# Three of the four activation sums of Strassen's forms on GpSimd, with two signs turned

## The chip, the cores and the metric

The kernel runs as one launch on one core of a Trainium2 chip. The time is the device time of a launch in microseconds (us), the median of 3 runs. The engines are written as in the profile: PE is TensorE (matmuls), DVE VectorE, ACT ScalarE, POOL GpSimd, SP SyncE, which here only issues transfers.

## The reference

One decoder block in float32, depth 1, batch 1: 512 tokens of width 1024, 256 memory tokens, a feed-forward width of 2816.

```python
def swiglu(u, w_gate_up, w_down):
    gate, up = jnp.split(u @ w_gate_up, 2, axis=-1)
    return (jax.nn.silu(gate) * up) @ w_down

    h = h + hybrid_mixer(rmsnorm(h, mix_norm[l]), ...)          # SSD heads + causal pooling
    h = h + memory_cross_attention(rmsnorm(h, xattn_norm[l]), rmsnorm(mem, mem_norm[l]), ...)
    h = h + swiglu(rmsnorm(h, ffn_norm[l]), w_gate_up[l], w_down[l])
    return rmsnorm(h, final_norm)
```

The change is in the feed-forward part alone, the last two fifths or so of the launch (from about 455 us on).

## The kernel before

**Precision.** Each float32 product is made of three passes in the PE's fp32r type: high part by high part, low by high, high by low. For a weight quad of 128x1024, ACT casts the high part (`whi`, L203) and DVE subtracts it from the quad for the low part (`wlo`, L205). Activations are split in the same way.

**Strassen.** The feed-forward products use Strassen's seven block products. For each pair of 128-channel blocks an activation set consists of FA and FB, 128x512 each: FA holds x11 (columns 0 to 255, `lo_`) and x12 (`hi_`), the first 256 tokens of the two blocks; FB holds x21 and x22, the other 256 tokens. `forms` (L1174) makes the seven left-hand forms of a set from them, each as a high and a low part:

- forms 1 and 2 are x11 and x12 as they are: high part `H1` (ACT, tile t_xh), low part `L1` (DVE L1193, t_xl);
- M, tile t_x57, holds form 5 = x11 - x21 (L1189) and form 7 = x22 - x21 (L1190), with `H2` and `L2` as its parts;
- N, tile t_x64, holds form 6 = -M_lo - x22 (L1197) and form 4 = -N_lo - x12 (L1199), with `H3` and `L3`;
- form 3 is x22: `H4`, tile t_xq, with its low part in the second half (L1184).

`forms` is called for 15 sets: i = 0 to 3 from the output projection of the attention (`i_o`, L1054 fills FA and FB), i = 4 to 14 from the gated values (`i_turnff`: PE transposes into a PSUM tile ffT, ACT copies FB and FA out of it, L1167).

**Stages.** The feed-forward work goes through gate/up blocks g (U:0 to U:5; matmul outputs gA, gB, gC) and down blocks d (d:0 to d:2; outputs dA, dB, dC) in the order g:0, g:1, d:0, g:2, g:3, d:1, g:4, g:5, d:2. A down block needs the sets of the two gate/up blocks ahead of it; the last of these sets are made while the down block already runs: i = 6 and 7 in d:0, 10 and 11 in d:1, 13 and 14 in d:2. The products within a block run in the order 1, 2, 5, 6, 3, 7, 4. After each product the PSUM result is added to its target: by DVE into the residual tiles t_hT in a down block (L1259), by ACT and DVE into t_gu tiles in a gate/up block, where ACT applies SiLU (L1118).

**Weights.** Four quads of each block matrix lie in memory; the seven weight forms are sums of them. For f = 5 and f = 7 a base quad is loaded on SP (L161, `raw<-w_s`) and a second one is added to it by a transfer that accumulates, issued on POOL (L172, `raw<-w_s`), which waits for the base to land. For f = 6 such a transfer on POOL adds one tile to another (L211, `wq<-raw`), for f = 3 and some f = 6 DVE does it (L194). There are six `raw` buffers, so a base load also waits until the tile that was in its buffer before has been read. Weights are cast and split one slot of the plan ahead of the products that use them.

**Order.** A list of slots (`SPEC`) sets which products, sets and weights belong together. Within that, the framework's scheduler fixes one list of instructions per engine ahead of the launch; an engine works through its list strictly from the top, and an instruction that waits holds up all behind it. Before the change POOL runs 66 instructions: a few fills at the start and 56 transfers that accumulate (38 at L172, 18 at L211).

Of the kernel before, what the change touches and what calls it, by code (L numbers as in the profile page):

```python
# [7 lines left out]
F32 = mybir.dt.float32  # L8
F32R = mybir.dt.float32r
AF = mybir.ActivationFunctionType  # L10
ALU = mybir.AluOpType
# [24 lines left out]

START = "x0 q0 h0 x1 h1 H0 q1 x2 x6 x3 q2 h2 q3 x4 q4 H1 q6 H2 q5 q7 a1 r0 x7 x5"
START_MM = "00 10 11 01 12 02 03 20 21 13 22 23 04 14 24 05 r 15 25 06 16 26 07 17 27"
# [23 lines left out]
def hybrid_block(ctx: ExitStack, tc: tile.TileContext, a: dict, out: bass.AP,  # L62
                 act_bufs=69, la=1, wb=(6, 4, 5), eng="", dact=(0, 1), raw_n=6, warm=12, spec=None, start=START, smm=START_MM, hu=1, dbg=None):
    nc = tc.nc
# [11 lines left out]
    def nm(base):  # L76
        uid[0] += 1
        return f"{base}_{uid[0]}"

    def T(base, dt=F32, n=512):  # L80
        return act.tile([P, n], dt, tag="a", name=nm("t_" + base))
# [141 lines left out]
    def need(*key):  # L223
        while key not in st:
            yield
# [35 lines left out]
    st = {}  # L261
# [778 lines left out]
    def i_o(m):  # L1040
        it = Item(keys=[("o", m)])

        def mm():
            proj(hold(it, "wo"), ready[("o", m)], [st["o", k] for k in range(8)])

        def post():
            h = st["h1", m]
            nc.vector.tensor_tensor(out=h, in0=h, in1=it.ps, op=ALU.add)
            yield
            i, c = m // 2, m % 2  # L1050
            if c == 0:
                st["F", i] = T("fa"), T("fb")
            for k in range(2):
                nc.scalar.activation(st["F", i][k][:, 256 * c:256 * c + 256], h[:, 256 * k:256 * k + 256],  # L1054
                                     AF.Identity, scale=col(V_FFN + m))
            yield
            if c == 1:
                yield from forms("fg", i, *st["F", i])

        it.mm, it.post = mm, post  # L1060
        return it
# [47 lines left out]
    def i_gu(b, f, part=None):  # L1109
        it, ends, width = product("g", b, f, part)  # L1110

        def add(base, tt, k):
            g = st[base, tt][:, :width]
            st["drained"] = nc.vector.tensor_tensor(out=g, in0=g, in1=it.ps[tt], op=ALU.add)  # L1114
            return g

        def gate(g, c):
            st["silu"] = nc.scalar.activation(g, g, AF.Silu, scale=st["r3",][:, c:c + 1])  # L1118

        def post():  # L1120
            if f in (1, 6, 5):
                for tt in range(2):
                    t = st["up"[f == 5] + str(f), tt] = T("gu")
                    nc.scalar.copy(t[:, :width], it.ps[tt])
            elif f in (2, 3):
                base, k = ("u1", 0) if f == 2 else ("u6", 1)
                gs = [add(base, tt, k) for tt in range(2)]
                yield
                yield from need("r3")
                for tt in range(2):  # L1130
                    gate(gs[tt], 2 * k + tt)
                    st["gate", k, tt] = st[base, tt]
            elif f == 7:
                us = [add("p5", tt, 1) for tt in range(2)]
                yield
                for tt in range(2):
                    nc.vector.scalar_tensor_tensor(out=us[tt], in0=us[tt], scalar=st["nr3",][:, 2 + tt:3 + tt],
                                                   in1=st["gate", 1, tt][:, :width], op0=ALU.mult, op1=ALU.mult)
                    st["fft", b, 1, tt] = st["p5", tt]
            else:  # L1140
                for tt in range(2):
                    g = st["gate", 0, tt][:, :width]
                    st["drained"] = nc.vector.scalar_tensor_tensor(
                        out=g, in0=it.ps[tt], scalar=st["nr3",][:, tt:tt + 1], in1=g, op0=ALU.mult, op1=ALU.mult)
                    st["fft", b, 0, tt] = st["gate", 0, tt]
            yield

        it.post = post if ends else None
        return it

    def i_turnff(b, i):

        it = Item()

        def mm():
            it.ps = psum.tile([P, 1024], F32, tag="pd", name=nm("ffT"), bufs=1)
            for k in (1, 0):
                for c in range(2):
                    for tt in range(2):
                        o = 512 * k + 256 * c + P * tt  # L1160
                        nc.tensor.transpose(it.ps[:, o:o + P], st["fft", b, k, tt][:, (2 * i + c) * P:(2 * i + c + 1) * P],
                                            ident)

        def post():
            F = T("fa"), T("fb")
            for k in (1, 0):
                nc.scalar.copy(F[k], it.ps[:, 512 * k:512 * k + 512])  # L1167
            yield
            yield from forms("ff", 2 * b + i, *F)

        it.mm, it.post = mm, post
        return it

    def forms(x, i, FA, FB):  # L1174

        lo_, hi_ = slice(0, 256), slice(256, 512)

        def cast(base, src, w=None):
            h = T(base, F32R)
            nc.scalar.copy(h if w is None else h[:, w], src)  # L1180
            return h

        def rest(dst, src, h):
            nc.vector.tensor_tensor(out=dst, in0=src, in1=h.bitcast(F32), op=ALU.subtract)  # L1184

        H1 = cast("xh", FA)
        H4 = cast("xq", FB[:, hi_], lo_)
        M = T("x57")
        nc.vector.tensor_tensor(out=M[:, lo_], in0=FA[:, lo_], in1=FB[:, lo_], op=ALU.subtract)  # L1189
        nc.vector.tensor_tensor(out=M[:, hi_], in0=FB[:, hi_], in1=FB[:, lo_], op=ALU.subtract)  # L1190
        yield
        L1 = T("xl", F32R)
        st["first rest"] = nc.vector.tensor_tensor(out=L1, in0=FA, in1=H1.bitcast(F32), op=ALU.subtract)  # L1193
        st["X", x, 1, i], st["X", x, 2, i] = (H1[:, lo_], L1[:, lo_]), (H1[:, hi_], L1[:, hi_])
        H2 = cast("xh", M)
        N = T("x64")
        nc.vector.scalar_tensor_tensor(out=N[:, lo_], in0=M[:, lo_], scalar=-1.0, in1=FB[:, hi_],  # L1197
                                       op0=ALU.mult, op1=ALU.subtract)
        nc.vector.scalar_tensor_tensor(out=N[:, hi_], in0=N[:, lo_], scalar=-1.0, in1=FA[:, hi_],  # L1199
                                       op0=ALU.mult, op1=ALU.subtract)  # L1200
        yield
        H3 = cast("xh", N)
        L2 = T("xl", F32R)
        rest(L2, M, H2)
        st["X", x, 5, i], st["X", x, 7, i] = (H2[:, lo_], L2[:, lo_]), (H2[:, hi_], L2[:, hi_])
        yield
        rest(H4[:, hi_], FB[:, hi_], H4[:, lo_])
        st["X", x, 3, i] = H4[:, lo_], H4[:, hi_]
        L3 = T("xl", F32R)
        rest(L3, N, H3)  # L1210
        st["X", x, 6, i], st["X", x, 4, i] = (H3[:, lo_], L3[:, lo_]), (H3[:, hi_], L3[:, hi_])
# [31 lines left out]
        return it  # L1243


    INTO = {1: (0, 0, 1), 2: (0, 0, 1), 6: (0, 1, 1), 5: (1, 1, -1), 7: (1, 1, -1), 3: (0, 1, 1), 4: (1, 0, -1)}

    def i_down(p, f, part=None):
        it, ends, _ = product("d", p, f, part)

        def post():
            r, k, sign = INTO[f]
            last = p == 2
            if last and f == 2:
                st["pre"] = nc.scalar.preload_act_table_set("natural_log_exp_and_others")
                after(st["pre"], st["silu"])
            for tt in range(2):
                h = st["h", 2 * k + tt, r]
                st["drained"] = nc.vector.tensor_tensor(out=h, in0=h, in1=it.ps[tt],  # L1259
                                                        op=ALU.add if sign > 0 else ALU.subtract)  # L1260
                if last and f in (2, 3, 7, 4):
                    squares(2 * k + tt, r)
                if last and f == 2:
                    gain(tt)
                if last and f == 4:
                    final([tt])
            if last and f == 7:
                gain(2)
                gain(3)
                final([2, 3])  # L1270
            yield
# [239 lines left out]
```

## Time and profile before

| what | value |
|---|---|
| time, median of 3 runs | 794.72 us (794.49 to 794.93) |
| profiled execution, span | 793.5 us |
| PE busy | 782.1 us, 99% of the span, 3780 matmuls |
| DVE busy | 635.8 us, 80%, 945 instructions |
| ACT busy | 498.4 us, 63%, 799 instructions |
| POOL busy | 49.9 us, 6%, 66 instructions |
| transfers | 128.60 MB, 162 GB/s over the span |

The profiled execution's own time is its span, 793.5 us; the median of the unprofiled runs is 1.2 us above it. A group's row reads: line, engine, operation, output tile <- input tiles, shape, count | busy time in us, mean ns of one | idle time of the engine ahead of them and what ended it. A timeline row reads: start, duration, engine, line, operation; in brackets the idle time of the engine just before it and what ended that. Names there lack their numbers, so M and N both read t_x. A row of windows gives, for each engine, the busy us and the number of instructions in that stretch, then PE's granted clock (1.00 is full speed), the share of time that the DMA engines were busy, and GB/s.

### The profile page before, as it was taken

The page shows a single profiled execution, that of the slowest core. Times are in us where ns is not written, and L with a number is a line of the kernel's source. Part 1 is how long each engine was busy: PE and PEld are TensorE (multiplying, and loading weights), DVE is VectorE, ACT ScalarE, POOL GpSimd, SP SyncE. Part 2 cuts the span into 40 slices and gives each one's busy share as a digit, 9 for nine tenths or more (in the row PEclk, how much of TensorE's full clock was granted, in tenths as well). Part 3 has the DMA queues.
Part 4 walks back from the last instruction along what each step waited for, and adds up shares of the span by engine and source line. Part 5 has one row for each costly group of instructions (what it writes and reads, how often), then busy time and mean ns, then how long its engine had stood idle before and what let it go on. Part 6 is the DMA issues. An engine that isn't in the chain of part 4 may idle for free.

```text
span 793.5 us, 10440 instructions
## 1 busy us (share of the span) xinstructions
PE 782.1 (99%) x3780; PEld 655.1 (83%) x3780; DVE 635.8 (80%) x945; ACT 498.4 (63%) x799; POOL 49.9 (6%) x66
## 2 busy tenths in 40 slices
PE   9999999999999999999999999999999999999995
PEld 7888888888888888888888888888888888888984
DVE  7999879999885799875766667788867698868897
ACT  8667699557953547555655695665445575455845
POOL 0000000000000000000000001011101011101000
PEclk9999999999999999999999999999999999999998
DMA  9235225133475234775446268688879697869602
GB/s 331 91 112 184 109 82 179 54 111 122 162 257 171 84 107 150 170 198 163 134 116 153 60 154 222 171 243 166 239 157 291 163 251 172 245 154 272 165 14 106
DMA packets 41282, 128.60 MB, mean 162 GB/s; under 512 B 4864, under 2 KB 7296, under 8 KB 41232
## 3 DMA queue, kind: packets, MB, share of 16 engines
q1 hardware_dynamic: 33024, 99.30, 37.0%
q0 software_dynamic: 8064, 28.58, 20.1%
q8 instruction: 29, 0.48, 0.2%
q14 instruction: 21, 0.17, 0.1%
q10 hardware_dynamic: 144, 0.07, 0.1%
HBM read 116.63 MB, written 2.13 MB: 150 GB/s over the span
## 4 chain that ended last, share of the span: by engine, by line
PE 92%; DVE 5%; issue 1%; DMA 1%; ACT 0%; SPq 0%; DVEq 0%
PE gA L1102 15%; PE gB L1102 8%; PE dA L1102 5%; PE gC L1102 4%; PE dB L1102 2%; PE xbc L117 2%; PE xbc L119 2%; PE xbc L118 2%; PE vAB L1102 2%; PE k L889 2%; PE z L117 2%; PE z L119 2%; PE op L117 2%; PE z L118 2%; PE wo L119 2%; PE op L118 2%
## 5 line engine op out<-in xcount | busy, mean ns | idle before, releaser
L203 ACT CAST whi<-raw 128x1024 fp32r<-128x1024 f32 (+1 forms) x125 | 129.0, 1040 | 91.1 <-PE wo L118 11.8
L205 DVE TENSOR_TENSOR wlo<-raw,whi 128x1024 fp32r<-128x1024 f32 (+1 forms) x125 | 149.8, 1208 | 28.2 <-ACT whi L203 27.3
L203 ACT CAST whi<-wq 128x1024 fp32r<-128x1024 f32 (+1 forms) x76 | 77.4, 1028 | 74.6 <-PE dA L1102 17.8
L205 DVE TENSOR_TENSOR wlo<-wq,whi 128x1024 fp32r<-128x1024 f32 (+1 forms) x76 | 90.3, 1194 | 38.7 <-ACT whi L203 38.6
L172 POOL DMA_DIRECT2D raw<-w_s x38 | 32.8, 867 | 646.0 <-DMA raw<-w_s 486.4
L1102 PE MATMUL gA<-whi,t_xh 128*128 128x512 f32 (+1 forms) x192 | 71.8, 374 | 0.0
L1102 PE MATMUL gA<-wlo,t_xh 128*128 128x512 f32 (+1 forms) x192 | 71.4, 372 | 0.0
L1102 PE MATMUL gA<-whi,t_xl 128*128 128x512 f32 (+1 forms) x192 | 71.3, 371 | 0.0
L1102 PEld LDWEIGHTS gA<-whi,t_xh 128*128 128x128 f32 x192 | 36.2, 188 | 6.6 <-ACT whi L203 0.4
L1102 PEld LDWEIGHTS gA<-wlo,t_xh 128*128 128x128 f32 x192 | 36.2, 188 | 6.3
L1102 PEld LDWEIGHTS gA<-whi,t_xl 128*128 128x128 f32 x192 | 36.2, 188 | 6.1
L1118 ACT ACTIVATE t_gu<-t_gu,s 128x512 f32<-128x512 f32 (+1 forms) x24 | 16.4, 688 | 35.9 <-DVE t_gu L1114 35.8
L194 DVE TENSOR_TENSOR wq<-wq,wq 128x1024 f32<-128x1024 f32 (+1 forms) x19 | 22.5, 1194 | 17.7 <-DMA wq<-raw 17.7
L1102 PE MATMUL dA<-whi,t_xh 128*128 128x512 f32 x88 | 34.1, 392 | 0.3 <-DVE t_hT L1259 0.2
L1102 PE MATMUL dA<-whi,t_xl 128*128 128x512 f32 x88 | 34.3, 389 | 0.0
L1102 PE MATMUL dA<-wlo,t_xh 128*128 128x512 f32 x88 | 34.1, 389 | 0.0
L1102 PE MATMUL gB<-whi,t_xq 128*128 128x512 f32 (+1 forms) x96 | 27.5, 371 | 0.0
L1180 ACT CAST t_xh<-t_x 128x512 fp32r<-128x512 f32 x30 | 18.6, 621 | 10.6 <-DVE t_x L1199 6.4
L117 PE MATMUL wo<-t_oh,whi 128*128 128x512 f32 x64 | 25.2, 394 | 0.0
L117 PE MATMUL v<-t_uh,whi 128*128 128x512 f32 x64 | 25.1, 392 | 0.0
L117 PE MATMUL z<-t_uh,whi 128*128 128x512 f32 x64 | 25.1, 392 | 0.0
L117 PE MATMUL q<-t_hgh,whi 128*128 128x512 f32 x64 | 25.1, 392 | 0.0
(401 smaller groups left out, 2221.2 us busy)
## 6 DMA issues: line engine op xcount, KB each, us to landing
raw<-w_u SPq DMA_DIRECT2D x68, 512.0 KB, 3.4
raw<-w_s SPq DMA_DIRECT2D x54, 512.0 KB, 4.6
wq<-w_s SPq DMA_DIRECT2D x36, 512.0 KB, 5.9
raw<-w_s POOLq DMA_DIRECT2D x36, 512.0 KB, 7.5
wq<-raw POOLq DMA_DIRECT2D x17, 512.0 KB, 8.6
t_x<-xT SPq DMA_DIRECT2D x16, 256.0 KB, 5.4
t_abc<-d_acs SPq DMA_DIRECT2D x16, 256.0 KB, 4.6
out<-t_hT SPq DMA_DIRECT2D x8, 256.0 KB, 2.3
```

The source lines that it names most:

```text
L117: nc.tensor.matmul(ps, whi, xhi, start=start, stop=False)
L118: nc.tensor.matmul(ps, whi, xlo, start=False, stop=False)
L119: nc.tensor.matmul(ps, wlo, xhi, start=False, stop=stop)
L172: nc.gpsimd.dma_start(sw[c, f][:, :n], quad("11" if f == 7 else "22"), accum_op=ALU.add)
L194: add = nc.vector.tensor_tensor(out=sw[c, 3][:, :n], in0=sw[c, 3][:, :n], in1=sw[c, 6][:, :n], op=ALU.add)
L203: nc.scalar.copy(hi[:, :n], raw[:, :n])
L205: nc.vector.tensor_tensor(out=lo[:, :n], in0=raw[:, :n], in1=hi.bitcast(F32)[:, :n], op=ALU.subtract)
L889: nc.tensor.matmul(it.ps[d], wh[:, ws], both, start=k == 0, stop=False, skip_group_check=True)
L1102: nc.tensor.matmul(it.ps[tt], p[:, ts_], w[:, ws], start=first, stop=(c, i, n) == pairs[-1] and p is xh and w is wl, skip_group_check=True)
L1118: st["silu"] = nc.scalar.activation(g, g, AF.Silu, scale=st["r3",][:, c:c + 1])
L1180: nc.scalar.copy(h if w is None else h[:, w], src)
```

## The change

`forms` has GpSimd make M_lo, M_hi and N_lo (L1187 to L1189 of the changed kernel); DVE keeps N_hi (now L1198), the low parts L1 (now L1195), L2, L3, and that of form 3 (now L1206). A plain subtraction gives N_lo only if M_lo is turned round, so form 5 is now x21 - x11, and form 3 is -x22 (ACT scales by -1 while it casts, L1192). The signs are taken back where the products are added up: `add` subtracts for f = 3 and f = 7 (its two other callers), the gate of f = 7 is multiplied by `r3` in place of its negative, and `INTO` turns the signs of 5 and 3. The tiles of M and N are also allocated ahead of those of H1 and H4. Nothing else is computed in another way. DVE's list goes from 937 rows to 892, POOL's from 71 to 116, ACT's and SP's keep their number (these lists count rows that a profile does not).

```diff
--- before.py
+++ after.py
@@ -1111,7 +1111,7 @@
 
         def add(base, tt, k):
             g = st[base, tt][:, :width]
-            st["drained"] = nc.vector.tensor_tensor(out=g, in0=g, in1=it.ps[tt], op=ALU.add)
+            st["drained"] = nc.vector.tensor_tensor(out=g, in0=g, in1=it.ps[tt], op=ALU.add if f == 2 else ALU.subtract)
             return g
 
         def gate(g, c):
@@ -1134,7 +1134,7 @@
                 us = [add("p5", tt, 1) for tt in range(2)]
                 yield
                 for tt in range(2):
-                    nc.vector.scalar_tensor_tensor(out=us[tt], in0=us[tt], scalar=st["nr3",][:, 2 + tt:3 + tt],
+                    nc.vector.scalar_tensor_tensor(out=us[tt], in0=us[tt], scalar=st["r3",][:, 2 + tt:3 + tt],
                                                    in1=st["gate", 1, tt][:, :width], op0=ALU.mult, op1=ALU.mult)
                     st["fft", b, 1, tt] = st["p5", tt]
             else:
@@ -1175,27 +1175,26 @@
 
         lo_, hi_ = slice(0, 256), slice(256, 512)
 
-        def cast(base, src, w=None):
+        def cast(base, src):
             h = T(base, F32R)
-            nc.scalar.copy(h if w is None else h[:, w], src)
+            nc.scalar.copy(h, src)
             return h
 
         def rest(dst, src, h):
             nc.vector.tensor_tensor(out=dst, in0=src, in1=h.bitcast(F32), op=ALU.subtract)
 
+        M, N = T("x57"), T("x64")
+        nc.gpsimd.tensor_tensor(out=M[:, lo_], in0=FB[:, lo_], in1=FA[:, lo_], op=ALU.subtract)
+        nc.gpsimd.tensor_tensor(out=M[:, hi_], in0=FB[:, hi_], in1=FB[:, lo_], op=ALU.subtract)
+        nc.gpsimd.tensor_tensor(out=N[:, lo_], in0=M[:, lo_], in1=FB[:, hi_], op=ALU.subtract)
         H1 = cast("xh", FA)
-        H4 = cast("xq", FB[:, hi_], lo_)
-        M = T("x57")
-        nc.vector.tensor_tensor(out=M[:, lo_], in0=FA[:, lo_], in1=FB[:, lo_], op=ALU.subtract)
-        nc.vector.tensor_tensor(out=M[:, hi_], in0=FB[:, hi_], in1=FB[:, lo_], op=ALU.subtract)
+        H4 = T("xq", F32R)
+        nc.scalar.activation(H4[:, lo_], FB[:, hi_], AF.Copy, scale=-1.0)
         yield
         L1 = T("xl", F32R)
         st["first rest"] = nc.vector.tensor_tensor(out=L1, in0=FA, in1=H1.bitcast(F32), op=ALU.subtract)
         st["X", x, 1, i], st["X", x, 2, i] = (H1[:, lo_], L1[:, lo_]), (H1[:, hi_], L1[:, hi_])
         H2 = cast("xh", M)
-        N = T("x64")
-        nc.vector.scalar_tensor_tensor(out=N[:, lo_], in0=M[:, lo_], scalar=-1.0, in1=FB[:, hi_],
-                                       op0=ALU.mult, op1=ALU.subtract)
         nc.vector.scalar_tensor_tensor(out=N[:, hi_], in0=N[:, lo_], scalar=-1.0, in1=FA[:, hi_],
                                        op0=ALU.mult, op1=ALU.subtract)
         yield
@@ -1204,7 +1203,8 @@
         rest(L2, M, H2)
         st["X", x, 5, i], st["X", x, 7, i] = (H2[:, lo_], L2[:, lo_]), (H2[:, hi_], L2[:, hi_])
         yield
-        rest(H4[:, hi_], FB[:, hi_], H4[:, lo_])
+        nc.vector.scalar_tensor_tensor(out=H4[:, hi_], in0=FB[:, hi_], scalar=-1.0, in1=H4.bitcast(F32)[:, lo_],
+                                       op0=ALU.mult, op1=ALU.subtract)
         st["X", x, 3, i] = H4[:, lo_], H4[:, hi_]
         L3 = T("xl", F32R)
         rest(L3, N, H3)
@@ -1243,7 +1243,7 @@
         return it
 
 
-    INTO = {1: (0, 0, 1), 2: (0, 0, 1), 6: (0, 1, 1), 5: (1, 1, -1), 7: (1, 1, -1), 3: (0, 1, 1), 4: (1, 0, -1)}
+    INTO = {1: (0, 0, 1), 2: (0, 0, 1), 6: (0, 1, 1), 5: (1, 1, 1), 7: (1, 1, -1), 3: (0, 1, -1), 4: (1, 0, -1)}
 
     def i_down(p, f, part=None):
         it, ends, _ = product("d", p, f, part)
```

The scheduler answers with another order. The place at which the prediction looks most is the set i = 6 at the start of d:0 (t_fa_1111_5197 and t_fb_1112_5198 are its FA and FB; set i = 7 is t_fa_1127_5249 and t_fb_1128_5250). First DVE, before:

```order
L205 TENSOR_TENSOR wlo_1139_5275<-wq_1098_5096,whi_1138_5274 128x1024
L1189 TENSOR_TENSOR t_x57_1117_5208<-t_fa_1111_5197,t_fb_1112_5198 128x256
L1190 TENSOR_TENSOR t_x57_1117_5208<-t_fb_1112_5198 128x256
L1193 TENSOR_TENSOR t_xl_1118_5212<-t_fa_1111_5197,t_xh_1115_5204 128x512
L1197 SCALAR_TENSOR_TENSOR t_x64_1120_5216<-t_x57_1117_5208,t_fb_1112_5198 128x256
L1184 TENSOR_TENSOR t_xq_1116_5206<-t_fb_1112_5198,t_xq_1116_5206 128x256
L1199 SCALAR_TENSOR_TENSOR t_x64_1120_5216<-t_x64_1120_5216,t_fa_1111_5197 128x256
L205 TENSOR_TENSOR wlo_1147_5316<-raw_1101_5104,whi_1146_5315 128x1024
L1184 TENSOR_TENSOR t_xl_1122_5221<-t_x57_1117_5208,t_xh_1119_5214 128x512
```

and now, with the start of set i = 7 at its end:

```order
L205 TENSOR_TENSOR wlo_1139_5275<-wq_1098_5096,whi_1138_5274 128x1024
L1198 SCALAR_TENSOR_TENSOR t_x64_1116_5205<-t_x64_1116_5205,t_fa_1111_5197 128x256
L205 TENSOR_TENSOR wlo_1147_5316<-raw_1101_5104,whi_1146_5315 128x1024
L1195 TENSOR_TENSOR t_xl_1119_5214<-t_fa_1111_5197,t_xh_1117_5209 128x512
L1206 SCALAR_TENSOR_TENSOR t_xq_1118_5211<-t_fb_1112_5198,t_xq_1118_5211 128x256
L1184 TENSOR_TENSOR t_xl_1122_5221<-t_x57_1115_5204,t_xh_1120_5216 128x512
L1184 TENSOR_TENSOR t_xl_1123_5224<-t_x64_1116_5205,t_xh_1121_5219 128x512
L205 TENSOR_TENSOR wlo_1150_5338<-wq_1075_4994,whi_1149_5337 128x1024
L1198 SCALAR_TENSOR_TENSOR t_x64_1132_5257<-t_x64_1132_5257,t_fa_1127_5249 128x256
L1195 TENSOR_TENSOR t_xl_1135_5266<-t_fa_1127_5249,t_xh_1133_5261 128x512
```

The one sum that DVE keeps (N_hi, L1198) now stands at the head of its set, ahead of a weight's low part (wlo_1147) and of L1 (t_xl_1119); before, L1 stood third in its set, and N_hi last.

POOL at the same place, before:

```order
L211 DMA wq_1075_4994<-raw_1092_5057 128x1024
L211 DMA wq_1095_5064<-raw_1101_5104 128x1024
L172 DMA raw_1166_5439<-w_s 128x1024
L172 DMA raw_1169_5446<-w_s 128x1024
L172 DMA raw_1184_5553<-w_s 128x1024
L172 DMA raw_1187_5560<-w_s 128x1024
```

and now:

```order
L211 DMA wq_1075_4994<-raw_1092_5057 128x1024
L211 DMA wq_1095_5064<-raw_1101_5104 128x1024
L172 DMA raw_1166_5439<-w_s 128x1024
L1187 TENSOR_TENSOR t_x57_1115_5204<-t_fb_1112_5198,t_fa_1111_5197 128x256
L1188 TENSOR_TENSOR t_x57_1115_5204<-t_fb_1112_5198 128x256
L1189 TENSOR_TENSOR t_x64_1116_5205<-t_x57_1115_5204,t_fb_1112_5198 128x256
L1188 TENSOR_TENSOR t_x57_1131_5256<-t_fb_1128_5250 128x256
L172 DMA raw_1169_5446<-w_s 128x1024
L1187 TENSOR_TENSOR t_x57_1131_5256<-t_fb_1128_5250,t_fa_1127_5249 128x256
L1189 TENSOR_TENSOR t_x64_1132_5257<-t_x57_1131_5256,t_fb_1128_5250 128x256
L172 DMA raw_1184_5553<-w_s 128x1024
```

The transfers keep their order. The three sums of set i = 6 stand behind the accumulation into raw_1166, and two of the sums of set i = 7 behind the one into raw_1169. At d:1 the lists have the same shape, with the sets i = 10 and 11.

ACT's list changes at this place too: the casts of M and N (H2, H3) of a set now follow each other, ahead of the cast of whi_1149 and of the copies of the next set's FB and FA. On PE the six dB matmuls of set i = 6 (form 5) now stand ahead of the dA and dC matmuls of set i = 7.

## The prediction

> **What bounds the kernel now.** I read the page first: busy times and the chain of work that ended last.
>
> ```profile
> PE 782.1 (99%) x3780; PEld 655.1 (83%) x3780; DVE 635.8 (80%) x945; ACT 498.4 (63%) x799; POOL 49.9 (6%) x66
> PE 92%; DVE 5%; issue 1%; DMA 1%; ACT 0%; SPq 0%; DVEq 0%
> ```
>
> PE is busy for 782.1 of 793.5 us, and the chain runs through it for 92%. Next, all that PE waits for in the whole span (columns: us in total, times, longest):
>
> ```profile
> PE warm L384 <- DVE ones L100: 1.2, 1, 1.2
> PE s L117 <- ACT whi L130: 0.8, 1, 0.8
> PE yo L119 <- DVE t_prl L241: 0.4, 1, 0.4
> PE dA L1102 <- DVE t_hT L1259: 0.2, 1, 0.2
> ```
>
> Where the change acts (L1102) PE waits for 0.2 us in all. So time taken off DVE buys at most 0.2 us there, plus what the tail behind the last matmul gives; anything that reaches PE too late costs its full lateness. Third, stretches: the end of gate/up blocks g:2 and g:3, the starts of d:0 and d:1, and the middle of d:2.
>
> ```profile
> 506.00:545.00 39.00, 39.00 (x190) 32.60 (x189) 33.24 (x48) 28.71 (x42) 5.13 (x6) 1.00 0.89 230
> 545.00:565.00 20.00, 19.86 (x88) 16.11 (x87) 18.61 (x27) 9.46 (x12) 1.72 (x2) 1.00 0.73 169
> 664.00:684.00 20.00, 19.86 (x88) 16.14 (x87) 18.87 (x26) 9.66 (x12) 1.72 (x2) 1.00 0.71 179
> 764.00:770.00 6.00, 6.00 (x28) 4.97 (x27) 6.00 (x11) 3.87 (x7) 0.00 (x0) 1.00 0.00 0
> ```
>
> DVE (fourth figure) has 5.8 us free in the first, but only 1.4 and 1.1 us in the two starts and none in d:2. There a delay on DVE can't be made up.
>
> **What is removed and added.** Groups of DVE and POOL:
>
> ```profile
> L1193 DVE TENSOR_TENSOR t_xl<-t_fa,t_xh 128x512 fp32r<-128x512 f32 x15 | 10.3, 686 | 0.1
> L1189 DVE TENSOR_TENSOR t_x<-t_fa,t_fb 128x256 f32<-128x256 f32 x15 | 6.3, 420 | 1.2 <-ACT t_fa L1167 0.9
> L172 POOL DMA_DIRECT2D raw<-w_s x38 | 32.8, 867 | 646.0 <-DMA raw<-w_s 486.4 <-DVE t_p L997 54.0 <-DVE t_hT L1259 38.7
> L109 POOL TENSOR_SCALAR_AFFINE_SELECT cmask<-cmask 128x128 f32<-128x128 f32 x1 | 0.3, 289 | 0.0
> L1503 POOL MEMSET const-float32-0.0<- 128x1 f32 x1 | 0.1, 100 | 0.3 <-issue 0.3
> ```
>
> DVE loses 45 sums of 420 ns (L1189 stands for the three lines): 18.9 us busy. They start 0.34 us apart (timelines below), so the real relief is 45 x 0.34 = 15.3 us, 1.0 us per set. By the second paragraph it is worth nothing, since PE's work covers it; only in d:2, where DVE never rests, could 1.0 us show.
>
> The trace has no GpSimd sum of two inputs. Lower bound: DVE's own 0.42 us. Upper: the select reads one input; less the 0.10 us of an almost empty POOL instruction it takes 0.19 us for 128 columns, or 0.48 us for 256 with the 0.10; a sum that reads its two inputs one after the other would take 0.10 + 2 x 0.38 = 0.86 us. I take 0.66, between the two; per set 3 x 0.66 + 0.1 for the links = 2.1 us. The Trainium skill (GPSIMD Engine Reference, Engine selection) advises against this very move: elementwise work of two inputs belongs on VectorE, GpSimd being about twice as slow. By its 2.6 cycles per element a sum would be about 0.65 us (an estimate from that page), and the total the same.
>
> **What is moved: sums behind transfers.** This decides. POOL works strictly in order, and the three sums of set 6 stand behind the accumulation into raw_1166; DVE's kept sum L1198 needs the last of them, and behind it on DVE wait the weight part wlo_1147 and L1. POOL around d:0, and SP's issues of the two base loads:
>
> ```profile
> 538.39 0.86 POOL L211 DMA_DIRECT2D wq<-raw  x1 [6.49 <-DVE wlo L205]
> 545.51 0.85 POOL L172 DMA_DIRECT2D raw<-w_s  x1 [6.26 <-DMA raw<-w_s]
> 548.74 0.86 POOL L172 DMA_DIRECT2D raw<-w_s  x1 [2.37 <-DVE t_x L1190]
> 539.76 0.33 SPq L161 DMA_DIRECT2D raw<-w_s  x1
> 543.87 0.33 SPq L161 DMA_DIRECT2D raw<-w_s  x1
> ```
>
> The accumulation at 545.51 waits for the base load issued at 539.76. That at 548.74 follows its base load (543.87) by 4.87 us too; the releaser in its bracket had long been done. Now what DVE does, and when PE reads it:
>
> ```profile
> 539.51 0.59 ACT L1167 COPY t_fa<-ffT 128x512 f32<-128x512 f32 x1
> 540.81 0.69 DVE L1193 TENSOR_TENSOR t_xl<-t_fa,t_xh 128x512 fp32r<-128x512 f32 x1
> 542.09 0.42 DVE L1199 SCALAR_TENSOR_TENSOR t_x<-t_x,t_fa 128x256 f32<-128x256 f32 x1
> 542.61 1.23 DVE L205 TENSOR_TENSOR wlo<-raw,whi 128x1024 fp32r<-128x1024 f32 x1
> 545.44 0.39 PE L1102 MATMUL dA<-whi,t_xl 128*128 128x512 f32 x1
> 545.66 0.39 PE L1102 MATMUL dA<-wlo,t_xh 128*128 128x512 f32 x1
> ```
>
> Before, L1 of set 6 is done at 541.50 and read at 545.44, and FA is there at 540.10. Now, at d:0:
>
> 1. POOL leaves its transfer at 545.51 + 0.85 = 546.4; the sums take until 548.5; L1198 runs to 549.0 (a step of 0.42 and a hand-over of 0.1); wlo_1147 starts then and holds DVE for 1.15 us (1.23 less the overlap); L1 ends at 549.0 + 1.15 + 0.69 = 550.85. PE wanted it at 545.44: **5.4 us**.
> 2. wlo_1147 also frees the buffer of raw_1169 (both orders: it reads raw_1101, and the row at 543.87 follows its end at 543.84). It now ends at 550.2 instead, so the base load is issued then and its accumulation at 550.2 + 4.87 = 555.1; POOL is free at 555.95, M_lo and N_lo of set 7 take 1.4, L1198 ends at 557.9, L1 of set 7 at 558.55. In PE's order 21 matmuls stand between the two L1; at 0.227 us (545.44 to 545.66 and on) PE would be there at 550.85 + 4.75 = 555.6: **3.0 us** more.
> 3. DVE is behind by then. PE's next tight place is a weight part in form 3:
>
> ```profile
> 558.75 2.35 DVE L205 TENSOR_TENSOR wlo<-wq,whi 128x1024 fp32r<-128x1024 f32 x2
> 560.02 0.50 PE L1102 MATMUL dB<-wlo,t_xq 128*128 128x512 f32 x1
> ```
>
>    The first of these two ends at 559.97 and is used at 560.02. From L1198 of set 7 (start 557.5) DVE's new list has up to its end 0.34 + 0.61 + 0.34 + 1.2 (that set), seven additions into t_hT at 0.6, two L194 and one other wlo at 1.15, and itself 1.22: 11.4 us, so 568.9, or 8.9 us late. The 8.4 us of steps 1 and 2 lie inside this. d:0 costs **9.0 us**.
>
> At d:1 the lists have the same shape:
>
> ```profile
> 664.79 0.85 POOL L172 DMA_DIRECT2D raw<-w_s  x1 [6.99 <-DMA raw<-w_s]
> 664.13 0.39 PE L1102 MATMUL dA<-whi,t_xl 128*128 128x512 f32 x1
> ```
>
> POOL is free 1.51 us after PE's need, against 0.92 at d:0, so every later step there lies 0.6 us further back: a first wait of 6.0 us, and a sum of **9.6 us**.
>
> PE's clock may add to this. Stretches of 1 us in the tail, where no matmul is left from 786 on:
>
> ```profile
> 786.00:787.00 1.00, 0.00 (x0) 0.00 (x0) 0.93 (x4) 0.81 (x3) 0.00 (x0) 1.00 0.90 338
> 787.00:788.00 1.00, 0.00 (x0) 0.00 (x0) 0.88 (x3) 0.97 (x4) 0.00 (x0) 0.76 1.00 387
> 788.00:789.00 1.00, 0.00 (x0) 0.00 (x0) 0.51 (x3) 0.36 (x2) 0.00 (x0) 0.50 0.96 377
> ```
>
> After 1 to 2 us without a matmul the granted clock falls to 0.76, then 0.50. A wait of 5.4 us is longer, so some matmuls behind it run at half speed. That loss falls before the second wait, which hides up to 3.0 us of it: nothing taken.
>
> The other sets. Sets 0 to 3 are made at 422 to 462 us and read by PE from 455 on: nothing. Set 4 stands behind
>
> ```profile
> 511.67 0.86 POOL L172 DMA_DIRECT2D raw<-w_s  x1 [2.16 <-DVE t_x L1189]
> ```
>
> so its L1198 ends at 512.5 + 2.1 + 0.5 = 515.1, where DVE before was done with the same sum at 513.4; DVE stands for up to 3.7 us, which its 5.8 us of rest (506 to 545) take up: 0, at most 1. Sets 8 and 9 likewise. For set 14 in d:2:
>
> ```profile
> 759.78 0.43 DVE L1189 TENSOR_TENSOR t_x<-t_fa,t_fb 128x256 f32<-128x256 f32 x1 [0.87 <-ACT t_fa L1167]
> 760.46 0.69 DVE L1193 TENSOR_TENSOR t_xl<-t_fa,t_xh 128x512 fp32r<-128x512 f32 x1
> 764.15 0.39 PE L1102 MATMUL dA<-whi,t_xl 128*128 128x512 f32 x1
> ```
>
> the sums start at 759.8 and end at 761.4 (M_hi needs FB alone and goes ahead), DVE loses 1.6 us and saves 1.0: **+0.5**, as it never rests behind.
>
> Sum: 793.5 + 9.0 + 9.6 + 0.5 = 812.6 for the profiled span; with the 1.2 us between span and median **814 us**. With sums of 0.42 or 0.86 us, five of them lie in each chain: -1.2 or +1.0 us per down block. With the doubt on set 4 the case's own range is 810 to 818.
>
> **The rivals.**
>
> - *Only the first wait counts* (15%). If the second base load goes out earlier (its buffer freed otherwise) and DVE catches up, there remain 5.4 + 6.0 + 0.5: 806.6, say 804 to 810. Against it: the rows 542.61 and 543.87 fit to 0.03 us.
> - *GpSimd and DVE shut each other out* (10%). If a GpSimd sum and a DVE subtraction of two tiles can't run together, each of the 45 sums holds DVE, or waits for up to one wlo (1.2 us). While L1198 waits DVE is idle anyway; there remain M_hi of set 7 and of set 11 (up to 1.2 us each) and the last sets in d:2, where DVE would pay 2.0 us per set (13 and 14): 814 + 2.4 + 4 = 820, if all of it shows. The trace has no two-input sum on POOL to judge by. The Trainium skill (SBUF — State Buffer, on the shared port pair) states such an exclusive lock for a DVE instruction with two SBUF inputs against a GpSimd one that reads SBUF.
> - *No change* (8%). If POOL's sums ran at once when FA lands (540.1), N_lo would be there at 542.3, L1198 at 542.7, L1 of set 6 at 544.6, still ahead of 545.44: 794.7. It needs POOL's transfer not to hold up what stands behind it. For it: POOL is 6% busy. Against it: every POOL row follows the landing that it waits for, none overtakes.
> - *Faster* (5%). The sums of sets 13 and 14 come in time, and DVE keeps 1.0 us of each in d:2, where it has no rest and its last additions stand behind the last matmul: 794.7 - 2.0 = 792.7. It decides only if d:0 and d:1 pass without a wait, so it needs what the case before it needs as well.
>
> **How the numbers follow.** Forecast 62%, the rivals 15, 10, 8 and 5%. What this kernel's timing can tell from no change is about 0.2%, 1.6 us. Slower: 62 + 15 + 10 = 87%; within: 8%; faster: 5%. The range from 800 to 821 leaves out the last two cases, 13%, and a few per cent for what is dearer still; its lower end takes in a first wait half as long at both places (793.5 + 2.7 + 3.0 + 1.2 = 800.4).
>
> **What would show it.** Right: PE waits of 5 to 6 us at dA L1102 for t_xl (L1195) soon after 545, a second one of some 3 us about 10 us later, the same pair at d:1; DVE idle ahead of L1198, released by POOL L1189; POOL's L1187 right behind its L172; a granted clock below 1.00 there; sums of 0.4 to 0.9 us; DVE near 617 us busy. Wrong: POOL's accumulations issued before 541, L1198 ending before 544, or PE waits under 1 us. A sum of well over 0.9 us, or DVE subtractions longer than 687 ns for 128x512, would mean the lock.

## The result and the profile after

The changed kernel takes 818.84 us (817.72 to 820.47, 4 runs) against 794.63 us (794.49 to 794.93, 4 runs) of the kernel before, measured together: a ratio of 1.0305, 95% interval 1.0291 to 1.0318. That is 24.2 us slower. The forecast was 814, with a range of 800 to 821 and 87% on slower. One of the four runs of e3 (below) took 1320.53 us at a granted clock of 0.556, and what is said of e3 goes by the other three.

The page's busy times and chain, after:

```profile
PE 788.9 (97%) x3780; PEld 658.3 (81%) x3780; DVE 622.0 (76%) x900; ACT 499.2 (61%) x799; POOL 85.5 (10%) x111
PE 78%; DMA 7%; DVE 7%; issue 3%; POOL 3%; ACT 2%; SPq 0%; POOLq 0%; DVEq 0%; ACTq 0%
```

DVE did get lighter, by 13.8 us (635.8 to 622.0), and POOL heavier by 35.6. PE runs the same 3780 matmuls, yet 14% of the chain have gone from PE to transfers, POOL, DVE, ACT and issue. All that PE waits for at the block products and the transposes ahead of them (columns as in the prediction):

```profile
PE dA L1102 <- DVE t_xl L1195: 10.5, 2, 5.7
PE gA L1102 <- DVE t_gu L1114: 4.6, 3, 1.8
PE dA L1102 <- DVE wlo L205: 1.0, 1, 1.0
PE hT L1220 <- ACT t_hT L1224: 0.8, 1, 0.8
PE gA L1102 <- DVE wlo L205: 0.5, 1, 0.5
PE dB L1102 <- DVE wlo L205: 0.4, 1, 0.4
```

Before, this was one row of 0.2 us. Together the rows are 17.8 us; the rest of the 24.2 lies in PE's own busy time, which grew by 6.8 us for the same matmuls, most of it behind the two largest waits, where the granted clock was down (last section). The largest row is the one that was forecast: 4.8 and 5.7 us at dA for L1 (now L1195). POOL at d:0, after:

```profile
549.44 0.85 POOL L172 DMA_DIRECT2D raw<-w_s  x1 [5.90 <-DMA raw<-w_s]
550.00 1.04 POOL L1187 TENSOR_TENSOR t_x<-t_fb,t_fa 128x256 f32<-128x256 f32 x1
550.69 1.03 POOL L1188 TENSOR_TENSOR t_x<-t_fb 128x256 f32<-128x256 f32 x1
551.37 1.02 POOL L1189 TENSOR_TENSOR t_x<-t_x,t_fb 128x256 f32<-128x256 f32 x1
555.01 1.10 POOL L1188 TENSOR_TENSOR t_x<-t_fb 128x256 f32<-128x256 f32 x1 [2.62 <-ACT t_fb L1167]
558.17 0.88 POOL L172 DMA_DIRECT2D raw<-w_s  x1 [2.06 <-DVE wlo L205]
```

The first sum starts right behind the accumulation, which waited 5.90 us for its base load; the three end at 552.39, 2.10 us after POOL was done with the transfer (550.29). Then DVE and PE:

```profile
552.43 0.43 DVE L1198 SCALAR_TENSOR_TENSOR t_x<-t_x,t_fa 128x256 f32<-128x256 f32 x1 [7.96 <-POOL t_x L1189]
552.77 1.22 DVE L205 TENSOR_TENSOR wlo<-raw,whi 128x1024 fp32r<-128x1024 f32 x1
553.90 0.68 DVE L1195 TENSOR_TENSOR t_xl<-t_fa,t_xh 128x512 fp32r<-128x512 f32 x1
560.67 0.42 DVE L1198 SCALAR_TENSOR_TENSOR t_x<-t_x,t_fa 128x256 f32<-128x256 f32 x1 [2.88 <-POOL t_x L1189]
570.75 2.36 DVE L205 TENSOR_TENSOR wlo<-wq,whi 128x1024 fp32r<-128x1024 f32 x2
```

```profile
554.64 0.80 PE L1102 MATMUL dA<-whi,t_xl 128*128 128x512 f32 x1 [4.80 <-DVE t_xl L1195]
572.02 0.50 PE L1102 MATMUL dB<-wlo,t_xq 128*128 128x512 f32 x1 [0.43 <-DVE wlo L205]
683.72 0.80 PE L1102 MATMUL dA<-whi,t_xl 128*128 128x512 f32 x1 [5.68 <-DVE t_xl L1195]
```

DVE stands for 7.96 us at the sum that it kept, and L1, which needs nothing of POOL, comes behind it.

Where the 24 us arose can be read by setting the start of each matmul against the start of the same matmul before (the pairs at the ends of the stretches stand in the fences of the prediction and above: 560.02 and 572.02, say, are one matmul). The lateness was 0.2 us up to the output projection and then

| stretch | lateness at its end, us | gained there |
|---|---|---|
| sets 0 to 3, gate/up blocks 0 and 1 (to 475 us of before) | 1.15 | 1.0 |
| g:2, in which sets 4 and 5 are made (to 545) | 4.25 | 3.1 |
| d:0 (to 562) | 12.0 | 7.75 |
| g:3, sets 8 and 9 (to 650) | 13.7 | 1.7 |
| d:1 (to 682) | 22.1 | 8.3 |
| the rest, sets 12 to 14 (to 785) | 23.75 | 1.7 |

### The profile page after: what moved, and what is told of

Read it like the earlier page. It is cut to its first block, busy times and chain, and to the rows that moved or that the text cites. A ratio compares the mean times of both kernels' runs of the same rounds, so it can differ in the third digit from the quotient of the medians.

```text
span 817.2 us, 10472 instructions
## 1 busy us (share of the span) xinstructions
PE 788.9 (97%) x3780; PEld 658.3 (81%) x3780; DVE 622.0 (76%) x900; ACT 499.2 (61%) x799; POOL 85.5 (10%) x111
## 4 chain that ended last, share of the span: by engine, by line
PE 78%; DMA 7%; DVE 7%; issue 3%; POOL 3%; ACT 2%; SPq 0%; POOLq 0%; DVEq 0%; ACTq 0%
PE gA L1102 9%; PE dA L1102 5%; PE gB L1102 5%; DMA wq<-raw 3%; DMA raw<-w_s 3%; PE gC L1102 3%; PE xbc L119 2%; PE xbc L118 2%; PE xbc L117 2%; DVE wlo L205 2%; PE dB L1102 2%; PE vAB L1102 2%; PE z L117 2%; PE k L889 2%; PE z L119 2%
## 5 line engine op out<-in xcount | busy, mean ns | idle before, releaser
L1102 PE MATMUL dA<-whi,t_xl 128*128 128x512 f32 x88 | 35.6, 404 | 10.5 <-DVE t_xl L1195 10.5
L1198 DVE SCALAR_TENSOR_TENSOR t_x<-t_x,t_fa 128x256 f32<-128x256 f32 x15 | 6.4, 425 | 43.3 <-POOL t_x L1189 43.3
L1102 PEld LDWEIGHTS dA<-whi,t_xl 128*128 128x128 f32 x88 | 17.0, 193 | 14.9 <-DVE t_xl L1195 11.5
```

The source lines that it names most:

```text
L1102: nc.tensor.matmul(it.ps[tt], p[:, ts_], w[:, ws], start=first, stop=(c, i, n) == pairs[-1] and p is xh and w is wl, skip_group_check=True)
```

## Experiments

The sets are numbered through from 0 to 14, as above; the code counts those of the gated values from 0 again, so `("ff", 2)` is set 6. Theory A is the prediction's: what costs is where the GpSimd sums stand, behind accumulations that wait for base loads and ahead of a kept sum that holds up DVE.

**e1, the signs alone.** All sums on DVE, everything else as changed:

```diff
-        nc.gpsimd.tensor_tensor(out=M[:, lo_], in0=FB[:, lo_], in1=FA[:, lo_], op=ALU.subtract)
-        nc.gpsimd.tensor_tensor(out=M[:, hi_], in0=FB[:, hi_], in1=FB[:, lo_], op=ALU.subtract)
-        nc.gpsimd.tensor_tensor(out=N[:, lo_], in0=M[:, lo_], in1=FB[:, hi_], op=ALU.subtract)
+        nc.vector.tensor_tensor(out=M[:, lo_], in0=FB[:, lo_], in1=FA[:, lo_], op=ALU.subtract)
+        nc.vector.tensor_tensor(out=M[:, hi_], in0=FB[:, hi_], in1=FB[:, lo_], op=ALU.subtract)
+        nc.vector.tensor_tensor(out=N[:, lo_], in0=M[:, lo_], in1=FB[:, hi_], op=ALU.subtract)
```

> All 15 sets sum on DVE again; the turned signs, ACT's cast with scale -1, DVE's low part of form 3 and the earlier allocation of M and N stay. Theory A (what costs is where the GpSimd sums stand in POOL's list, behind accumulations that wait for base loads): the time is that of before, 794.7 us, within 1 us, and PE waits under 1 us in all at the block products (L1102). Rival B (the turned signs, the scaled cast or the new allocation order carry part of it): 2 us or more above before.

Measured: 794.20 us against 795.09, ratio 0.9990 (0.9981 to 0.9999). All the lateness is gone, and PE waits for nothing at the block products. Its whole list of waits:

```profile
PE warm L384 <- DVE ones L100: 1.2, 1, 1.2
PE s L117 <- ACT whi L130: 0.5, 1, 0.5
PE yo L119 <- DVE t_prl L241: 0.4, 1, 0.4
```

Rival B falls: signs, the scaled cast and the allocation order cost nothing.

**e2 and e3, by sets.** In e2 GpSimd sums only for sets 6, 7, 10 and 11, in e3 (`not in`) only for the other eleven; the two lines behind change alike:

```diff
+        eng = nc.gpsimd if (x, i) in (("ff", 2), ("ff", 3), ("ff", 6), ("ff", 7)) else nc.vector
-        nc.gpsimd.tensor_tensor(out=M[:, lo_], in0=FB[:, lo_], in1=FA[:, lo_], op=ALU.subtract)
+        eng.tensor_tensor(out=M[:, lo_], in0=FB[:, lo_], in1=FA[:, lo_], op=ALU.subtract)
...
```

> GpSimd sums for only the four sets 6, 7, 10 and 11, those that stand behind an accumulation at d:0 and d:1; the other eleven sum on DVE. Theory A: the two first waits (about 5 to 6 us each) and the half clock behind them remain. PE's lateness grew by 8.5 us over d:0 and by 8.3 us over d:1 in the changed kernel, so 794.7 + 17 = 811.5, within 2 us. Rival C (a GpSimd sum costs the same wherever it stands, by its duration or by shutting DVE out): 4 of 15 sets give 4/15 of 24.2 us, 801.

> The converse: sets 6, 7, 10 and 11 sum on DVE, the other eleven on GpSimd. Theory A: d:0 and d:1 lose their waits of 5 us; what is left is the lateness that grew over gate/up blocks 0 to 2 (3.5 us), block 3 (1.7 us) and the rest to the end (2.0 us): 794.7 + 7 = 802, within 2.5 us. Rival C: 11 of 15 sets give 17.7 us, 812.

Measured: e2 810.93 us (ratio 1.0198, 1.0182 to 1.0213), e3 803.07 us (801.52 to 804.08; 1.0098, 1.0080 to 1.0115). Four sets cost 15.8 us, the other eleven 8.0; together 23.8, nearly the whole. The same instruction is more than five times as dear in one place as in the other (4.0 us a set against 0.7), so rival C (a price per sum) falls. The largest row of e2's PE waits is the one of the full change:

```profile
PE dA L1102 <- DVE t_xl L1195: 12.0, 3, 6.5
```

**e4 and e5, all sums on GpSimd, but ahead of the accumulations.** The edits order POOL's list alone. `st["pool sum"]` is the last N_lo; the condition shown is e4's, that of e5 is `f == 5 and "pool sum" in st`:

```diff
-            nc.gpsimd.dma_start(sw[c, f][:, :n], quad("11" if f == 7 else "22"), accum_op=ALU.add)
+            acc = nc.gpsimd.dma_start(sw[c, f][:, :n], quad("11" if f == 7 else "22"), accum_op=ALU.add)
+            if f == 5 and CHUNKS[c][:2] in (("g", 2), ("g", 4)):
+                after(acc, st["pool sum"])
```

> All three sums of all 15 sets stay on GpSimd; only the order of POOL's list changes: the accumulations that stood ahead of the sums of sets 6, 7, 10 and 11 now stand behind them. Theory A: the same 45 GpSimd sums with the same durations, but no wait of 5 us at d:0 and d:1: as without GpSimd there, 802, within 2.5 us. Rival C (duration of the sums or the lock): nothing gained, 815 to 819.

> As the kernel with the accumulations behind the sums of sets 6, 7, 10 and 11 (805.7 us), and now every accumulation for form 5 behind the sums that come before it in the program, so those at sets 4 and 8 too. That kernel lost 1.7 us ahead of form 4 of gate/up block 2 and 1.7 us at block 3, where PE waits for DVE's addition into t_gu (L1114). Theory A1 (POOL's accumulation ahead of sets 4 and 8 made DVE and ACT late there): these 3.4 us go, 802 within 1.5 us. Rival D (it is the longer chain FB, GpSimd, DVE, ACT of each set, with its hand-overs, whatever stands on POOL): 805 to 806, nothing gained.

Measured: e4 805.66 us (1.0147, 1.0121 to 1.0174), e5 802.73 us (1.0097, 1.0082 to 1.0112). The same 45 sums on the same engine cost 13 us less with four of their sets moved ahead of four transfers, and 16 less with every accumulation for form 5 behind the sums. In e4 the sums of set 6 run as soon as FB is there, the accumulations (L170 here) follow, and PE's waits for L1 (second fence) shrink from 10.5 to 2.0 us:

```profile
542.28 1.13 POOL L1188 TENSOR_TENSOR t_x<-t_fb 128x256 f32<-128x256 f32 x1 [0.41 <-ACT t_fb L1167]
550.71 0.87 POOL L170 DMA_DIRECT2D raw<-w_s  x1
```

```profile
PE gA L1102 <- DVE t_gu L1114: 4.5, 3, 1.7
PE dA L1102 <- DVE t_xl L1195: 2.0, 2, 1.0
```

The scheduler answered in other lists too, alike in e4 and e5. At d:0 and d:1 the weight part that stood between the kept sum and L1 now stands behind the set's low parts, and PE's dA and dC matmuls of set 7 (and of set 11) stand earlier again. DVE at d:0 in e4:

```profile
544.95 0.43 DVE L1198 SCALAR_TENSOR_TENSOR t_x<-t_x,t_fa 128x256 f32<-128x256 f32 x1 [2.15 <-POOL t_x L1189]
545.29 0.68 DVE L1195 TENSOR_TENSOR t_xl<-t_fa,t_xh 128x512 fp32r<-128x512 f32 x1
547.43 1.22 DVE L205 TENSOR_TENSOR wlo<-raw,whi 128x1024 fp32r<-128x1024 f32 x1
```

So the 13 us are the price of the place on POOL together with what the scheduler makes of it; between e4 and e5 POOL's list alone differs. By the medians e5 took 2.9 of the 3.4 us that theory A1 gave it. The traces show less, and not at both places: the spans differ by 1.6 us (802.6 and 801.0), the wait at block 2 fell from 1.69 to 0.32 us, the one at block 3 only from 1.74 to 1.56. So rival D holds for block 3, where sums that start right behind FB leave the wait nearly as it was, and the lateness of the gate/up blocks has two causes.

**e6, L1 ahead of the kept sum on DVE.**

```diff
-        nc.vector.scalar_tensor_tensor(out=N[:, hi_], in0=N[:, lo_], scalar=-1.0, in1=FA[:, hi_],
-                                       op0=ALU.mult, op1=ALU.subtract)
+        nhi = nc.vector.scalar_tensor_tensor(out=N[:, hi_], in0=N[:, lo_], scalar=-1.0, in1=FA[:, hi_],
+                                             op0=ALU.mult, op1=ALU.subtract)
+        after(nhi, st["first rest"])
```

> The changed kernel (818.8 us) with one order on DVE: L1 (L1195) ahead of the kept sum N_hi (L1198) in each set. Theory A as the prediction's third step has it (what sets the end of d:0 and d:1 is DVE's lateness, which starts where the kept sum waits for POOL): the first wait at L1 goes, but H2, L2 and the weight parts behind the kept sum stay late; 1 to 4 us gained per down block, 811 to 817. Rival E (it is L1 behind the kept sum that costs): all 17 us of d:0 and d:1 gained, 802.

Measured: 813.87 us (1.0231, 1.0211 to 1.0251), 5 us better. Rival E falls: the two waits for L1 are gone, and others stand in their place, for what lies behind the kept sum (L1179 casts H1 to H3 in this kernel, L1183 makes L2 and L3):

```profile
PE dB L1102 <- DVE t_xl L1183: 2.7, 3, 0.9
PE dA L1102 <- ACT t_xh L1179: 1.7, 2, 0.9
PE dB L1102 <- ACT t_xh L1179: 1.4, 2, 1.1
```

**e7 and e8, the other sets by themselves.** As e2, with `("ff", 0), ("ff", 1), ("ff", 4), ("ff", 5)` in e7 (sets 4, 5, 8, 9) and `("ff", 8), ("ff", 9), ("ff", 10)` in e8 (sets 12 to 14).

> GpSimd sums only for sets 4, 5, 8 and 9 (made in gate/up blocks 2 and 3), DVE sums the rest. Theory A: the lateness of those blocks alone, about 1.8 us each and up to 1 us that follows from it: 794.5 + 4.5 = 799, within 1.5 us. Rival: what blocks 2 and 3 lose is an after-effect of the sets 0 to 3 on GpSimd: under 1 us, 795.

> GpSimd sums only for sets 12, 13 and 14 (gate/up block 5 and d:2), where DVE has no rest. Theory A (a set on GpSimd makes DVE wait longer than it saves): the 1.1 us at block 5 and the 1.0 us in d:2 remain, 796.5 within 1 us. Rival F (relief of DVE where it is the tightest): 3 x 1.0 us less on DVE, 792 to 793.5.

Measured: e7 798.44 us (1.0052, 1.0033 to 1.0071), e8 796.19 us (1.0014, 1.0005 to 1.0024), against 794.80. Both come out as theory A had them. e8 matters for the other sign: where DVE is at its tightest, taking 3 us of sums off it made the kernel 1.4 us slower by the medians, by the waits that the full change shows there too:

```profile
PE gA L1102 <- DVE t_gu L1114: 1.1, 1, 1.1
PE dA L1102 <- DVE wlo L205: 1.0, 1, 1.0
```

Together the parts make 15.8 (e2) + 3.6 (e7) + 1.4 (e8) = 20.8 of 24.2 us; the rest, 3.4, would be sets 0 to 3 (1.0 by the table) and what late parts do to each other. It was not measured by itself.

**e9, every GpSimd sum twice.**

```diff
+        for _ in range(2):
-        nc.gpsimd.tensor_tensor(out=M[:, lo_], in0=FB[:, lo_], in1=FA[:, lo_], op=ALU.subtract)
+            nc.gpsimd.tensor_tensor(out=M[:, lo_], in0=FB[:, lo_], in1=FA[:, lo_], op=ALU.subtract)
...
```

> The changed kernel (818.8 us) with each of the 45 GpSimd sums issued twice into the same tile. Theory A with its price term (each GpSimd sum that stands between an accumulation and the kept sum puts its length on the path): 4 more sums of 0.7 us lie in the chain of each of d:0 and d:1 (three for set 6, one more behind the second accumulation for set 7), 2 x 2.9; sets 4, 5, 8 and 9 are 2.1 us later each, which puts 2 to 4 us on each of gate/up blocks 2 and 3; 1 to 2 at the end: 830 us, within 4. Rival G (only the wait for the transfer counts, the sums lie beside other work): 819 to 821.

Measured: 847.31 us (1.0658, 1.0643 to 1.0673), 28.5 us above the changed kernel. Rival G falls, but so does my size: 830 was expected. The comparison has a second difference, too: with the doubled sums the scheduler puts L1 ahead of the kept sum, and the lists of DVE and ACT are those of e6. Against e6 (813.87 us) the 45 x 0.7 = 31.5 us of added GpSimd time cost 33.4, more than their length. Some 20 of that are waits of PE (33.0 us in all at the block products and the transposes, 12.5 in e6), the largest of them for ACT. Some 12 are PE's own busy time, 801.0 us against 788.9, at a granted clock of 0.979 over the span against 0.994:

```profile
PE 801.0 (95%) x3780; PEld 663.4 (79%) x3780; DVE 633.7 (75%) x900; ACT 498.8 (59%) x799; POOL 123.1 (15%) x156
PE dB L1102 <- ACT t_xh L1179: 7.6, 4, 3.1
PE gA L1102 <- ACT t_gu L1124: 7.2, 2, 3.6
```

Read as in the table, every stage lost 4.5 to 7.9 us more than in e6. So POOL has little slack left in any of them, and the way to PE often leads through ACT. ACT in g:2 of the changed kernel shows why:

```profile
515.14 0.62 ACT L1180 CAST t_xh<-t_x 128x512 fp32r<-128x512 f32 x1 [2.65 <-POOL t_x L1187]
516.42 0.63 ACT L1180 CAST t_xh<-t_x 128x512 fp32r<-128x512 f32 x1 [0.66 <-DVE t_x L1198]
516.95 0.58 ACT L1124 COPY t_gu<-gB 128x512 f32<-128x512 f32 x1
519.80 0.60 ACT L1167 COPY t_fb<-ffT 128x512 f32<-128x512 f32 x1
```

The casts of M and N wait for POOL and for the kept sum, and the copies behind them take the products out of PSUM and bring the next set's FB. Before, that FB copy ran here:

```profile
515.84 0.60 ACT L1167 COPY t_fb<-ffT 128x512 f32<-128x512 f32 x1
```

so set 5 began 4.0 us late (1.15 of it was there already), went through POOL and DVE again, and the addition into t_gu that frees a bank for PE came late:

```profile
533.95 0.47 PE L1102 MATMUL gA<-whi,t_xh 128*128 128x512 f32 x1 [1.83 <-DVE t_gu L1114]
```

**e10, accumulations behind the sums and L1 ahead of the kept sum** (the edits of e5 and e6).

> GpSimd keeps its 45 sums; the accumulations for form 5 stand behind them (802.7 us alone), and L1 stands ahead of the kept sum on DVE. Theory A: the two waits of 1.0 us at L1 of sets 7 and 11 go, what remains are the waits for t_gu at blocks 2, 3 and 5 and the one of 1.0 us in d:2: 800.5 within 1.5 us, still slower than before (794.8). Rival H (with both orders mended nothing is left but the relief of DVE): 792 to 795.

Measured: 800.72 us (1.0074, 1.0060 to 1.0088), as expected in total, though the waits for L1 shrank to 1.4 us and did not vanish. With both orders mended, GpSimd's sums still cost 5.7 us against before. The longer chain of a set, from ACT to POOL to DVE and back to ACT, would explain it, but no run changes that chain alone. Rival H falls. A variant that takes H3 off ACT's list was not tried.

**e11, the signs alone once more.**

> The turned signs with all sums on DVE once more, against the kernel before, with more rounds: 794.2 against 795.1 us in the first comparison, ratio 0.999 with an interval that just leaves 1 out. If the difference is there: 0.998 to 0.9995; if it was chance: an interval that holds 1.

Measured: 794.14 us against 795.04, ratio 0.9991 (0.9982 to 1.0000). Twice the same 0.1% less, at the edge of what can be told, and the one version here that is not slower than before. Where it comes from was not followed up.

## Why the prediction was right

The time lies inside the range, the sign and the mechanism were right, and the total was 5 us short. It is nearer than its parts by luck: d:0 and d:1 were forecast 2.5 us too dear (18.6 against 16.05), all other places 7 us too cheap (0.5 against 7.5), and the two errors partly cancel. By the steps of the prediction:

- **What bounds the kernel.** Right: 13.8 us less on DVE bought nothing. e8 shows it at its sharpest, in the very stretch where DVE never rests.
- **The price of a sum.** 0.66 us was taken, between 0.42 and 0.86; three in a row took 2.10 us, as worked out, and one that stands alone lasts 0.74. The rule of the Trainium skill (GPSIMD Engine Reference, Engine selection: elementwise work of two inputs belongs on VectorE) is borne out: 0.69 us against DVE's 0.34 from start to start.
- **Step 1, the first wait.** 5.4 us were forecast at d:0 and 6.0 at d:1; the rows show 4.80 and 5.68. POOL, L1198, the weight part and L1 followed each other as written, to 0.2 us once the 3.9 us by which all of it came late is taken off.
- **Step 2, the second base load.** The accumulation came 4.2 us after the weight part's end (4.87 forecast) and the kept sum of set 7 at 560.67. No PE wait shows there: between the two reads of L1, at 554.64 and 561.82, PE took 7.2 us instead of 4.75, because its clock was down. The prediction's sentence that this loss and the second wait would cover each other is what happened; so the second wait of some 3 us, which it named as a sign of being right, does not stand in the list of waits. The window behind the wait (the number ahead of the last two is the granted clock):

```profile
556.00:560.00 4.00, 4.00 (x11) 3.06 (x10) 1.80 (x2) 0.54 (x3) 1.86 (x4) 0.55 0.33 92
```

- **Step 3, DVE's lateness.** The weight part of form 3 was to be used 9.0 us late; of the 12.0 us at 572.02 the 4.25 from before d:0 come off: 7.75. At d:1 8.3 against 9.6. Both terms were 1.3 us too large. The larger part lies in the time from the weight part's end to the accumulation: 4.2 us at d:0 and, by the two rows below, 3.8 at d:1, where 4.87 were taken from one row. At d:1 PE did not wait at form 3: the first wait and the slow clock behind it already make the 8.3 us, and the weight part (the first of the two at 699.46) ended at 700.68, 0.05 us before its use at 700.73. There the two chains came out level, and the rows can't tell which of them sets the time. e6 bears the step out at d:0: with the first wait gone and no fall of the clock, the lateness, read as in the table, still grew by 5.5 us. Over d:1 it grew by 6.2 in e6, but there the clock did fall (last section).

```profile
681.84 1.22 DVE L205 TENSOR_TENSOR wlo<-raw,whi 128x1024 fp32r<-128x1024 f32 x1
686.87 0.88 POOL L172 DMA_DIRECT2D raw<-w_s  x1 [1.68 <-DVE wlo L205]
699.46 2.36 DVE L205 TENSOR_TENSOR wlo<-wq,whi 128x1024 fp32r<-128x1024 f32 x2
700.73 0.50 PE L1102 MATMUL dB<-wlo,t_xq 128*128 128x512 f32 x1
```

- **The other sets: the step that failed.** "0, at most 1" for set 4, the same for 8 and 9, and nothing for 0 to 3 were far too low: 1.0 + 3.1 + 1.7 us. The times forecast for set 4 were right: L1198 ended at 516.39, 1.15 us of lateness included, against 515.1, and DVE stood for 3.92 us (row below), where up to 3.7 were taken. What failed was the price put on that wait. The estimate asked whether DVE's free time in the stretch could take up its wait. It did not ask what ACT would do: its casts of M and N now waited for POOL and DVE, with the next set's copies and the copies out of PSUM behind them. The change in ACT's list was described ahead of the prediction, but had no term in the sum.

```profile
515.96 0.43 DVE L1198 SCALAR_TENSOR_TENSOR t_x<-t_x,t_fa 128x256 f32<-128x256 f32 x1 [3.92 <-POOL t_x L1189]
```

- **d:2.** +0.5 was forecast for set 14; 1.7 us arose with sets 12 to 14, 1.1 of it at block 5, where no term stood.
- **Rivals.** "No change" and "faster" fell, the latter by e8 in its own place. "Only the first wait" fell too, though less clearly: with the slow clock behind it that wait makes 7.2 of the 7.75 us at d:0 and all 8.3 at d:1. But DVE did not catch up, as this rival needs, and in e6 most of the loss stays without the wait. "GpSimd and DVE shut each other out" holds in kind, in the changed kernel at a small price (below).

## What to carry over

An engine with little work may still have a list that stands still: look at what is ahead of the new instructions in its order and how long that waits, not at its busy share. And follow a moved value through every engine that reads it: each hand-over puts a wait into one more in-order list, and what stands behind it there may belong to something else. When work is taken off an engine that is not the bound, the most it can buy is what the bound now waits for on it; here that was 0.2 us.

## What the runs showed of the hardware

GpSimd and DVE held each other up where a sum met a subtraction of two tiles, in both directions. At set 7 of the changed kernel the second of two subtractions, which take 1.29 us as a pair, ran into M_hi (POOL 555.01 to 556.11): the pair took 1.83 us, and the one that met the sum lasted 1.23 instead of 0.69. In e4 (second fence) an M_hi took 1.71 us; alone such a sum takes 0.74.

```profile
554.84 1.83 DVE L1184 TENSOR_TENSOR t_xl<-t_x,t_xh 128x512 fp32r<-128x512 f32 x2
561.95 1.29 DVE L1184 TENSOR_TENSOR t_xl<-t_x,t_xh 128x512 fp32r<-128x512 f32 x2
```

```profile
547.54 1.71 POOL L1188 TENSOR_TENSOR t_x<-t_fb 128x256 f32<-128x256 f32 x1 [2.63 <-ACT t_fb L1167]
```

This agrees with the exclusive lock that the Trainium skill states (SBUF — State Buffer, on the shared port pair). In the changed kernel three DVE instructions were stretched so, by 0.5 to 0.8 us each; more did not meet a sum, since DVE mostly stood still while the sums ran. It can be dearer: in e9 an L1 subtraction that met the doubled sums of set 4 lasted 3.70 us in place of 0.69. It ended at 520.10, behind the fourth sum (second row; the first had started at 516.43). The one of set 8 lasted 3.82 us.

```profile
516.40 3.70 DVE L1195 TENSOR_TENSOR t_xl<-t_fa,t_xh 128x512 fp32r<-128x512 f32 x1 [0.17 <-ACT t_xh L1179]
518.53 1.02 POOL L1189 TENSOR_TENSOR t_x<-t_x,t_fb 128x256 f32<-128x256 f32 x1
```

The clock after a wait was a second price that the prediction had only in words. Behind the 5 us without matmuls at d:0 and at d:1 the granted clock was down (0.55 from 556 to 560 us), and at each place 12 matmuls ran 0.43 us apart in place of 0.23, some 2.4 us. Here that lay inside DVE's lateness: at d:0 PE still waited 0.43 us for the weight part of form 3, and at d:1 the two came out level. Shorter waits could lower the clock too. In e6 PE waited for 0.36, 0.92 and 0.83 us between 551 and 555.3, and the clock stayed at 1.00 (first row); at d:1 it waited for 1.06, 0.92 and 0.86 us between 678 and 683.2, and the clock fell to 0.50 (second row).

```profile
550.00:554.00 4.00, 2.72 (x11) 1.69 (x10) 2.36 (x5) 2.61 (x5) 1.51 (x3) 1.00 0.85 135
684.00:688.00 4.00, 4.00 (x10) 3.07 (x10) 2.23 (x5) 2.19 (x3) 1.66 (x3) 0.50 0.80 131
```
